# The output projection of a token mixer by seven half products in place of eight

## The chip, the cores and the metric

The kernel runs on one core of one Trainium2 chip. The metric is device time in microseconds (us) of one execution; the median of three runs before the change is 2330.8 us (2329.96 to 2331.77). Everything below counts on one core's engines: TensorE (PE, matmuls), VectorE (DVE), ScalarE (ACT), GpSimd (POOL), SyncE (SP, which issues the DMAs), and the DMA engines.

## The reference

Two layers of a streaming encoder, 512 tokens by 1024 channels in float32. Each layer is a feed-forward net (FFN), a token mixer, and another FFN, each with a norm before and after it. What the change touches is the end of the mixer:

```python
branches = jnp.stack([sb_out, conv_out, gla_out], axis=2)
branch_d = jnp.einsum('bsgw,gwd->bsgd', branches, w_branch)
gates = jax.nn.sigmoid(gate_logits.reshape(b, s, N_BRANCHES, D_MODEL))
merged = jnp.sum(gates * branch_d, axis=2)
return merged @ w_out
```

`merged` is 512 x 1024 and `w_out` 1024 x 1024. Then follow `x = x + rms_norm(m, norm_post[l, 1])` and the second FFN, whose last step is a product with `w_down` (2816 x 1024).

## The kernel before, in words

**Precision.** Each float32 operand is split into a high part (a cast to fp32r, on ScalarE) and a low part (the rest, a subtraction on VectorE). A product is three matmuls: high by high, high by low, low by high. In the names, `whi` and `wlo` are the parts of a weight tile that was loaded as `raw`, `dh` and `dl`, or `mh` and `ml`, those of the other operand. `mm_out` (line 296) issues the three matmuls for 128 tokens by 512 output columns.

**The order of the work.** Matmuls stay in the order of the code. On VectorE and ScalarE, instructions marked `pinned` keep their order among themselves; a scheduler places the rest around them. Each engine's queue is fixed when the kernel is built. `whi` and `wlo` have five buffers each; `raw` has three, each of which holds two loads of 512 KB; and a load is issued by SP, in its order, once its buffer's last reader is done.

**The end of the mixer.** `gates(1, cv, merge)` runs over eight tiles of 128 channels. For each one TensorE computes `gate` (24 matmuls, `proj_cols`) and then `pb` (12 matmuls); ScalarE makes `gs`, the sigmoid of `gate`; VectorE multiplies `pb` by `gs` (line 1210), and GpSimd adds the result to `acc`, the merged tile, which is the transposed operand: 128 channels by 512 tokens. `merge` then splits that tile into `mh` and `ml`. `out_proj` (line 301) multiplies by `w_out`: rows 0 to 511 of the weights (four tiles) one tile after the other into eight PSUM banks, 24 matmuls a tile, then the last four tiles token block by token block (`token(i)`). In that way the first token block's sums are complete early, and the norms of the first blocks run on VectorE and ScalarE while TensorE does the next ones (`Hand`, line 244). Behind the third block come the transposes `pt` of the first normed block for the next FFN.

**The down projection of the FFN** (`Down`, line 569) computes 16 of its 22 weight row tiles by a 2 x 2 block product in seven half products instead of eight. The tokens are halved (`R2` is 0 to 255, `R1` 256 to 511), as are the rows and the columns of the weights. Its table has, for each half product, the operand, the blocks of the weights that are loaded, and the PSUM banks:

```python
        ORDER = (("A12", ((1, 0),), "B"), ("A11", ((0, 0),), "A"), ("S3", ((0, 1), (1, 1)), "C"),
                 ("S2", ((0, 0),), "A"), ("A22", ((1, 0),), "C"), ("S1", ((1, 1),), "A"), ("S4", ((1, 1),), "A"))
```

A step is one half product for a pair of row tiles, 12 matmuls; with 16 tiles there are four steps of each kind (`PER`). `sums(p)` loads the weights of step p and forms its sums on VectorE; `parts(p)` splits both operands, on ScalarE (`dh`, `whi`) and VectorE (`dl`, `wlo`); `ahead()` does the sums of one step and the parts of the step before it. `run` keeps four steps ahead: after product p it prepares step p+4 and, when p was the last of its kind, copies the banks' partial results out (`tap`, ScalarE). The sums `kept` and the copies lie in the buffers of `xh` and `xl`, the stage's input, which is no longer needed then. `MIDDLE` are two ordinary tiles between the sixth and the seventh kind; `LAST` are four that are done token block by token block. `sum_tokens` forms sums of token halves as tiles come; `sum` adds the copied results to the banks at the end.

Of the kernel before, what the change touches and what calls it, by code (L numbers as in the profile page):

```python
# [9 lines left out]
F32R = mybir.dt.float32r  # L10
# [31 lines left out]
def kernel(  # L42
# [33 lines left out]
    def bank(n, tag="pb"):  # L76
        return psp.tile([P, 512], F32, tag=tag, name=n, bufs=BANKS[tag])
# [218 lines left out]
    def mm_out(o, t, sh, sl, wh, wl, st=False, en=False):  # L296
        mm(o, sh[:, t], wh, start=st, stop=False, skip_group_check=True)
        mm(o, sh[:, t], wl, start=False, stop=False, skip_group_check=True)
        mm(o, sl[:, t], wh, start=False, stop=en, skip_group_check=True)

    def out_proj(w2d, nk, stat, tail, finish, upcoming, early, head=None):


        ld = lambda k: load_rows(w2d, k)
        fresh = head is None
        if fresh:
            banks = [[bank(f"o{i}{h}", "pb" if i < 3 else "pa") for h in range(2)] for i in range(NT)]
        else:
            banks, rest = head

        def mms(i, h, k, sh, sl, wh, wl):
            mm_out(banks[i][h], slice(i * P, (i + 1) * P), sh, sl, wh[:, HS[h]], wl[:, HS[h]],
                   fresh and k == 0, k == nk - 1)

        for k in range(nk - tail if fresh else 0):
            wh, wl = ld(k)
            sh, sl = stat(k)
            for i in range(NT):
                for h in range(2):
                    mms(i, h, k, sh, sl, wh, wl)  # L320
        if fresh:
            rest = [(k, ld(k), stat(k)) for k in range(nk - tail, nk)]
        def token(i):
            for h in range(2):
                for k, (wh, wl), (sh, sl) in rest:
                    mms(i, h, k, sh, sl, wh, wl)

        if early is None:
            for i in range(NT):
                token(i)  # L330
                finish(i, banks[i])
            return None

        held[0] = True
        a, b, c, d = [finish(i, banks[i]) for i in range(NT)]
        forms = finish(None, None)
        w, steps = early()
        next(steps)
        token(0)
        a.half(0)  # L340
        a.half(1)
        a.mean()
        token(1)
        a.add()
        b.half(0)
        a.mean()
        b.sum(1)
        a.normal()
        b.square(1)
        b.scaled(1)  # L350
        b.mean()
        token(2)
        c.half(0)
        b.add()
        c.half(1)
        b.mean()
        c.mean()
        arrival(0, a.hns, forms)

        for k, (wh, wl), (sh, sl) in rest:  # L360
            for h in range(2):
                mms(NT - 1, h, k, sh, sl, wh, wl)
        next(steps)
        b.normal()
        for _ in steps:
            pass
        c.add()
        d.sum(0)
        d.sum(1)
        held[0] = False  # L370

        def second():
            held[0] = True
            arrival(1, b.hns, forms)
            held[0] = False
            d.square(0)
            d.square(1)
            c.mean()
            d.mean()
            c.normal()  # L380
            d.scaled(0)
            d.scaled(1)
            d.add()
            d.mean()
            d.normal()

        upcoming.extend((None, second, lambda: arrival(2, c.hns, forms), lambda: arrival(3, d.hns, forms)))
        return w
# [178 lines left out]


    class Down:
        F0, NP = 2, 8  # L570
        R1, R2 = slice(256, 512), slice(0, 256)
        PER = NP // 2

        ORDER = (("A12", ((1, 0),), "B"), ("A11", ((0, 0),), "A"), ("S3", ((0, 1), (1, 1)), "C"),
                 ("S2", ((0, 0),), "A"), ("A22", ((1, 0),), "C"), ("S1", ((1, 1),), "A"), ("S4", ((1, 1),), "A"))
        AHEAD = 4
        MIDDLE, LAST = (0, 1), (18, 19, 20, 21)

        def __init__(self, wd, hid):
            self.wd, self.hid = wd, hid  # L580
            self.ready = {}
            self.s1 = None
            self.next = 0
            self.raw = {}
            self.plan()
# [48 lines left out]
        def sums(self, p):  # L634

            self.load(p)
            j, c = self.steps[p]
            if j is None:
                return
            name, raws = self.ORDER[j][0], self.raw[p]  # L640
            tt = lambda o, a, b, op: pinned(nc.vector.tensor_tensor(o, a, b, op=op))
            kept = None if j < 2 else self.kept[:, 2 * c:2 * c + 2, :].rearrange("p k c -> p (k c)")
            src = raws[0]
            if name == "S3":
                tt(kept, raws[0], raws[1], ALU.subtract)
                src = kept
            if name == "S2":
                for q, x in enumerate(self.of(p)):
                    tt(x, self.s1[c][:, q], x, ALU.add)
                tt(kept, kept, raws[0], ALU.subtract)  # L650
                src = kept
            if name == "S4":
                for q, x in enumerate(self.of(p)):
                    tt(x, x, self.hid[self.F0 + 2 * c + q][:, self.R1], ALU.add)
            if name == "S1":
                pinned(nc.vector.scalar_tensor_tensor(src, kept, -1.0, raws[0], op0=ALU.mult, op1=ALU.subtract))
            if name == "A22":
                tt(src, kept, raws[0], ALU.add)
            self.raw[p] = src
# [40 lines left out]
                    t = slice(q * 256 + i * P, q * 256 + (i + 1) * P)  # L700
                    mm_out(b[i], t, sh, sl, hi[:, w], lo[:, w], st=(q == 0 and c == 0 and j < 3))

        def run(self, late):
            c0, d0, c1, d1, b0, b1 = (bank(n) for n in ("oC", "oD", "oC", "oD", "oB", "oB"))
            a0, a1 = (bank("oA", "pa") for i in range(2))
            self.banks = {"A": (a0, a1), "B": (b0, b1), "C": (c0, c1), "D": (d0, d1)}
            self.out = [[c0, d0], [c1, d1], [b0, a0], [b1, a1]]
# [9 lines left out]
            for p in range(self.end):  # L717
# [12 lines left out]
                if j == 5:  # L730
                    tap(self.u4, "A")
                    for i in range(2):
                        pinned(nc.vector.tensor_tensor(self.u4[i], p7[i], self.u4[i], op=ALU.subtract))

                    self.p1 = [slot("p1") for i in range(2)]
                    for i in range(2):
                        pinned(nc.scalar.copy(self.p1[i], p1[i]))
            while self.next < len(self.steps):
                self.ahead()
            rest = []  # L740
            for p in range(self.end, len(self.steps)):
                sh, sl, hi, lo = self.ready[p]
                rest.append((self.steps[p][1], (hi, lo), (sh, sl)))
            return self.out, rest

        def sum(self, i, h, bank_):

# [24 lines left out]
    def ffn(wg, wu, wd, weights, forms, arrive, finish, upcoming, early, late, begin):  # L772
# [72 lines left out]
        spare.clear()  # L845
        fs = list(range(3, NF))
        n = 7 * len(fs)
        down = Down(wd, hid)
        block_tiles(wg, wu, fs, forms, hid, between)
        head = down.run(late)  # L850
        return out_proj(wd, NF, None, TAIL, lambda i, b: finish(i, b, down.sum), upcoming, early, head)
# [2 lines left out]
    def mixer(l, wv, arrive, finish, upcoming, early):  # L854
# [489 lines left out]
                    nc.vector.tensor_tensor(ys[c], ys[c], s_, op=ALU.mult)  # L1344
                cv = branch_split(ys, "s")

        merged = []

        def merge(d):
            tag = "t" if d < 4 else "q"  # L1350
            mh, ml = slot("mh", F32R, tag), slot("ml", F32R, tag)
            split(mh, ml, acc[d])
            merged.append((mh, ml))

        for _ in gates(1, cv, merge):
            pass
        return out_proj(w_out[l], KC, lambda k: merged[k], TAIL, finish, upcoming, early)


    load_x(0)  # L1360
# [84 lines left out]
```

## Time and profile before

| | |
|---|---|
| median of 3 runs | 2330.8 us |
| profiled execution | 2330.92 us, its span 2329.2 us |
| TensorE, VectorE, ScalarE, GpSimd busy | 99%, 79%, 52%, 7% of the span |
| first matmul of the output projection | 781.8 us (layer 1) |
| its first 168 matmuls, as the chain shows them | 38.08 us |

A row of the groups has line, engine, operation, output<-inputs, shapes and count; behind the bar are the busy time, the mean of one in ns, and the idle time ahead of it with what ended it. A row of a time line has start and length in us. A row of waits has who waited for whom, the total, the number and the longest.

### The profile page before, as it was taken

The page shows a single profiled execution, that of the slowest core. Times are in us where ns is not written, and L with a number is a line of the kernel's source. Part 1 is how long each engine was busy: PE and PEld are TensorE (multiplying, and loading weights), DVE is VectorE, ACT ScalarE, POOL GpSimd, SP SyncE. Part 2 cuts the span into 40 slices and gives each one's busy share as a digit, 9 for nine tenths or more (in the row PEclk, how much of TensorE's full clock was granted, in tenths as well). Part 3 has the DMA queues.
Part 4 walks back from the last instruction along what each step waited for, and adds up shares of the span by engine and source line. Part 5 has one row for each costly group of instructions (what it writes and reads, how often), then busy time and mean ns, then how long its engine had stood idle before and what let it go on. Part 6 is the DMA issues. An engine that isn't in the chain of part 4 may idle for free.

```text
span 2329.2 us, 36177 instructions
## 1 busy us (share of the span) xinstructions
PE 2307.6 (99%) x14072; PEld 2057.9 (88%) x14072; DVE 1848.9 (79%) x2755; ACT 1221.7 (52%) x2370; POOL 165.0 (7%) x277
## 2 busy tenths in 40 slices
PE   8999999999999999999999999999999999999998
PEld 7999888887888899998899998888878888999987
DVE  7888987859965388889888889878599644888897
ACT  5555656644323255556555566566433333566664
POOL 0000001201021100000000000012010211000000
PEclk9999999999999999999999999999999999999999
DMA  5333644131333223336423336432313332333363
GB/s 173 91 109 109 218 161 119 55 100 52 109 91 109 82 73 99 101 109 225 155 82 100 109 110 235 149 110 60 95 55 109 91 92 81 89 99 104 114 221 109
DMA packets 332765, 265.33 MB, mean 114 GB/s; under 512 B 12747, under 2 KB 285165, under 8 KB 332593
## 3 DMA queue, kind: packets, MB, share of 16 engines
q1 hardware_dynamic: 332592, 263.02, 37.2%
q8 instruction: 110, 1.80, 0.3%
q14 instruction: 63, 0.51, 0.1%
HBM read 260.88 MB, written 2.10 MB: 113 GB/s over the span
## 4 chain that ended last, share of the span: by engine, by line
PE 97%; DVE 1%; ACT 1%; issue 0%; DMA 0%; SPq 0%; DVEq 0%; POOLq 0%; ACTq 0%
PE A L66 19%; PE gate L66 11%; PE C L66 9%; PE oA L66 9%; PE pb L66 6%; PE oC L66 5%; PE B L66 5%; PE o L66 3%; PE oB L66 3%; PE pf L66 3%; PE gr L66 2%; PE pa L66 2%; PE q L66 2%; PE gv L66 2%; PE pv L66 2%; PE pgl L66 2%
## 5 line engine op out<-in xcount | busy, mean ns | idle before, releaser
L455 DVE TENSOR_TENSOR wlo<-raw,whi 128x1024 fp32r<-128x1024 f32 (+1 forms) x304 | 331.0, 1089 | 108.7 <-ACT whi L453 107.9
L453 ACT CAST whi<-raw 128x512 fp32r<-128x512 f32 x532 | 315.3, 620 | 162.5 <-DVE raw L455 162.5
L115 ACT CAST whi<-raw 128x1024 fp32r<-128x1024 f32 (+2 forms) x178 | 185.0, 1045 | 351.3 <-PE gate L66 130.8
L116 DVE TENSOR_TENSOR wlo<-raw,whi 128x1024 fp32r<-128x1024 f32 (+2 forms) x178 | 223.0, 1261 | 173.2 <-ACT whi L115 168.5
L455 DVE TENSOR_TENSOR raw<-raw 128x512 f32<-128x512 f32 x304 | 209.1, 688 | 5.7
L66 PE MATMUL A<-xh,whi 128*128 128x256 f32 x608 | 172.5, 284 | 0.0
L66 PE MATMUL A<-xl,whi 128*128 128x256 f32 x608 | 172.0, 283 | 0.0
L66 PE MATMUL A<-xh,wlo 128*128 128x256 f32 x608 | 172.0, 283 | 0.0
L1030 DVE SCALAR_TENSOR_TENSOR y<-u,cw,y 128x511 f32<-128x511 f32 (+14 forms) x240 | 166.5, 753 | 0.0
L66 PE MATMUL gate<-xh,whi 128*128 128x512 f32 x384 | 151.3, 394 | 0.0
L66 PE MATMUL gate<-xh,wlo 128*128 128x512 f32 x384 | 149.8, 390 | 1.3 <-DVE wlo L116 1.3
L66 PE MATMUL gate<-xl,whi 128*128 128x512 f32 x384 | 149.6, 390 | 0.0
L671 ACT CAST whi<-raw 128x1024 fp32r<-128x1024 f32 x104 | 109.5, 1053 | 59.4 <-issue 16.9
L674 DVE TENSOR_TENSOR wlo<-raw,whi 128x1024 fp32r<-128x1024 f32 x104 | 126.6, 1217 | 17.3 <-ACT whi L671 17.3
L268 POOL TENSOR_TENSOR rs<-ms,mhalf 128x1 f32<-128x1 f32 x44 | 25.1, 576 | 1440.6 <-DVE ms L266 1440.6
L453 ACT COPY cp<-A 128x256 f32<-128x256 f32 x228 | 84.4, 370 | 68.5 <-PE A L66 67.6
L66 PE MATMUL oA<-wlo,dh 128*128 128x512 f32 x304 | 119.1, 392 | 0.0
L66 PE MATMUL oA<-whi,dh 128*128 128x512 f32 x304 | 118.4, 389 | 0.0
L66 PE MATMUL oA<-whi,dl 128*128 128x512 f32 x304 | 118.3, 389 | 0.0
L66 PEld LDWEIGHTS A<-xl,whi 128*128 128x128 f32 x608 | 116.5, 192 | 0.2
L66 PEld LDWEIGHTS A<-xh,whi 128*128 128x128 f32 x608 | 116.4, 191 | 0.2
L66 PEld LDWEIGHTS A<-xh,wlo 128*128 128x128 f32 x608 | 116.4, 192 | 0.0
(329 smaller groups left out, 7088.2 us busy)
## 6 DMA issues: line engine op xcount, KB each, us to landing
raw<-in_ffn_w_down_dram SPq DMA_DIRECT2D x152, 512.0 KB, 4.6
raw<-in_w_in_dram SPq DMA_DIRECT2D x108, 512.0 KB, 4.7
raw<-in_ffn_w_gate_dram SPq DMA_DIRECT2D x152, 256.0 KB, 3.4
raw<-in_ffn_w_up_dram SPq DMA_DIRECT2D x152, 256.0 KB, 4.6
raw<-in_w_branch_dram SPq DMA_DIRECT2D x24, 512.0 KB, 3.8
raw<-in_w_out_dram SPq DMA_DIRECT2D x16, 512.0 KB, 4.1
raw<-in_ffn_w_gate_dram SPq DMA_DIRECT2D x12, 512.0 KB, 4.9
raw<-in_ffn_w_up_dram SPq DMA_DIRECT2D x12, 512.0 KB, 4.5
```

Of the source, the lines that this page charges most:

```text
L66: tc.keep_in_program_order(nc.tensor.matmul(*a, **k))
L115: pin(nc.scalar.copy(hi, src))
L116: pin(nc.vector.tensor_tensor(lo, src, hi.bitcast(F32), op=ALU.subtract))
L268: nc.gpsimd.tensor_tensor(self.rs, ms, mhalf[:, 0:1], op=ALU.pow)
L453: copy = lambda o, i: pin(nc.scalar.copy(o, i))
L455: tt = lambda o, a, b, op: pin(nc.vector.tensor_tensor(o, a, b, op=op))
L671: pinned(nc.scalar.copy(hi, src))
L674: pinned(nc.vector.tensor_tensor(lo, src, hi.bitcast(F32), op=ALU.subtract))
L1030: nc.vector.scalar_tensor_tensor(y[:, back:], u[:, :S - back], cw[:, c, j:j + 1], y[:, back:], op0=ALU.mult, op1=ALU.add)
```

## The change

The mixer's output projection now uses `Down` for the first four of its eight row tiles of `w_out`: one step of each of the seven kinds (`NP` is 2, `PER` is 1), no `MIDDLE`, and tiles 4 to 7 as `LAST`. The split of each merged tile in `merge` is gone; in its place come sums of token halves at tiles 2 and 3, and one call of `ahead()` at tile 6. The other steps are prepared in `run`, behind the last gate tile. Since there is no middle tile, six matmuls of the first `LAST` tile are done ahead of the seventh product, and left out later. With one step of each kind, a second place in `kept` holds the later sums. Loads of `w_out` go from 8 to 12 a layer, and its matmuls from 192 to 180. The FFN's calls pass the old numbers.

```diff
-            banks, rest = head
+            banks, rest, done = head
 
         def mms(i, h, k, sh, sl, wh, wl):
+            if not fresh and k == done and i < 2 and h == 1:
+                return
...
     class Down:
-        F0, NP = 2, 8
...
-        PER = NP // 2
...
-        MIDDLE, LAST = (0, 1), (18, 19, 20, 21)
-
-        def __init__(self, wd, hid):
+
+        def __init__(self, wd, hid, f0, np, middle, last):
             self.wd, self.hid = wd, hid
+            self.F0, self.NP, self.PER = f0, np, np // 2
+            self.MIDDLE, self.LAST = middle, last
...
-            kept = None if j < 2 else self.kept[:, 2 * c:2 * c + 2, :].rearrange("p k c -> p (k c)")
+            kept = last = None
+            if j >= 2:
+
+                at = lambda n: self.kept[:, n:n + 2, :].rearrange("p k c -> p (k c)")
+                last = at(2 * c)
+                kept = at(2) if self.PER == 1 and j > 2 else last
...
-                tt(kept, kept, raws[0], ALU.subtract)
+                tt(kept, last, raws[0], ALU.subtract)
...
-        def run(self, late):
-            c0, d0, c1, d1, b0, b1 = (bank(n) for n in ("oC", "oD", "oC", "oD", "oB", "oB"))
+        def run(self, late, order=("C0", "D0", "C1", "D1", "B0", "B1")):
+            got = {n: bank("o" + n[0]) for n in order}
+            c0, d0, c1, d1, b0, b1 = (got[n] for n in ("C0", "D0", "C1", "D1", "B0", "B1"))
...
+                    if not self.MIDDLE:
+
+                        sh, sl, hi, lo = self.ready[self.end]
+                        for i in range(2):
+                            mm_out(self.out[i][1], slice(i * P, (i + 1) * P), sh, sl, hi[:, HS[1]], lo[:, HS[1]], st=True)
...
-        merged = []
+
+        down = Down(w_out[l], acc, 0, 2, (), (4, 5, 6, 7))
+        down.pairs()
 
         def merge(d):
-            tag = "t" if d < 4 else "q"
-            mh, ml = slot("mh", F32R, tag), slot("ml", F32R, tag)
-            split(mh, ml, acc[d])
-            merged.append((mh, ml))
+            for n in range(2):
+                down.sum_tokens(d, n)
+            if d == KC - 2:
+                down.ahead()
 
         for _ in gates(1, cv, merge):
             pass
-        return out_proj(w_out[l], KC, lambda k: merged[k], TAIL, finish, upcoming, early)
+        head = down.run(lambda: None, ("B0", "B1", "C0", "C1", "D0", "D1"))
+        return out_proj(w_out[l], KC, None, TAIL, lambda i, b: finish(i, b, down.sum), upcoming, early, head)
```

The order on VectorE around the last gate tile, before. Tile 7's weights are `raw_7606` in `wlo_7609`; `gs_7477` is tile 4's product, `gs_7528` tile 5's, `gs_7585` tile 6's and `gs_7637` tile 7's; the other `wlo` are those of `w_out`:

```order
L116 TENSOR_TENSOR wlo_7609<-raw_7606,whi_7608 128x1024 [waits DMAHW5_49,PE_49,Activation_49]
L1210 TENSOR_TENSOR gs_7477<-pb_7479,gs_7477 128x512 [waits PE_49,Activation_49]
L116 TENSOR_TENSOR ml_7495<-acc_6487,mh_7494 128x512 [waits Activation_49]
L116 TENSOR_TENSOR wlo_7668<-raw_7606,whi_7667 128x1024 [waits DMAHW6_49,PE_49,Activation_49]
L1210 TENSOR_TENSOR gs_7528<-pb_7530,gs_7528 128x512 [waits PE_49,Activation_49]
...
L1210 TENSOR_TENSOR gs_7585<-pb_7587,gs_7585 128x512 [waits PE_49,Activation_49]
L116 TENSOR_TENSOR ml_7603<-acc_6603,mh_7602 128x512 [waits Activation_49]
L116 TENSOR_TENSOR wlo_7757<-raw_7754,whi_7756 128x1024 [waits DMAHW1_49,PE_49,Activation_49]
L1210 TENSOR_TENSOR gs_7637<-pb_7639,gs_7637 128x512 [waits PE_49,Activation_49]
```

The same place now, up to the third product. `gs_7566` is tile 6's product and `gs_7627` tile 7's; `wlo_7599` are tile 7's weights; `dl_7587` and `wlo_7589` belong to the first half product (A12), `dl_7659` and `wlo_7661` to the second (A11); `xh_7652` is `kept`, written by the sums S3 and S2:

```order
L1222 TENSOR_TENSOR gs_7566<-pb_7568,gs_7566 128x512 [waits PE_49,Activation_49]
L679 TENSOR_TENSOR dl_7587<-acc_6334,dh_7586 128x256 [waits Activation_49]
L679 TENSOR_TENSOR dl_7587<-acc_6410,dh_7586 128x256 [waits Activation_49]
L680 TENSOR_TENSOR wlo_7589<-raw_7583,whi_7588 128x1024 [waits DMAHW5_49,Activation_49]
L116 TENSOR_TENSOR wlo_7599<-raw_7596,whi_7598 128x1024 [waits DMAHW7_49,Activation_49]
L1222 TENSOR_TENSOR gs_7627<-pb_7629,gs_7627 128x512 [waits PE_49,Activation_49]
L642 TENSOR_TENSOR xh_7652<-raw_7596,raw_7655 128x1024 [waits DMAHW1_49,DMAHW0_49]
L679 TENSOR_TENSOR dl_7659<-acc_6172,dh_7658 128x256 [waits Activation_49,Pool_49]
L679 TENSOR_TENSOR dl_7659<-acc_6247,dh_7658 128x256 [waits Activation_49]
L680 TENSOR_TENSOR wlo_7661<-raw_7583,whi_7660 128x1024 [waits DMAHW6_49,Activation_49]
```

Tile 7's `wlo` moved from ahead of tile 4's product to behind tile 6's, and the operands of the second half product stand behind tile 7's product.

On ScalarE, behind the last gate tile, casts of weights stood before, each for a tile of `w_out`:

```order
L115 CAST whi_7785<-raw_7754 128x1024 [waits DMAHW2_49,PE_49]
L115 CAST mh_7654<-acc_6658 128x512 [waits Pool_49]
L115 CAST whi_7791<-raw_7789 128x1024 [waits DMAHW3_49,DVE_49,PE_49]
L115 CAST whi_7796<-raw_7789 128x1024 [waits DMAHW4_49,DVE_49,PE_49]
L115 CAST whi_7802<-raw_7800 128x1024 [waits DMAHW5_49,DVE_49,PE_49]
```

Now the products' casts and the copies stand there. `whi_7711` is cast from the sum of A22, `whi_7737` from that of S1; `xl_7653` holds the copies (`tap`), first of the banks `oA` after the second product, then of the banks `oC` after the third:

```order
L676 CAST dh_7709<-acc_6334 128x256 [waits PE_49]
L676 CAST dh_7709<-acc_6410 128x256
L677 CAST whi_7711<-raw_7682 128x1024 [waits DMAHW3_49,DVE_49,PE_49]
L676 CAST dh_7735<-S1_7224 128x512
L677 CAST whi_7737<-raw_7682 128x1024 [waits DMAHW4_49,DVE_49,PE_49]
L720 COPY xl_7653<-oA_7650 128x512 [waits PE_49]
L720 COPY xl_7653<-oA_7651 128x512 [waits PE_49]
L676 CAST dh_7758<-acc_6334 128x256 [waits DVE_49]
L676 CAST dh_7758<-acc_6410 128x256 [waits DVE_49]
L677 CAST whi_7760<-raw_7731 128x1024 [waits DMAHW5_49,Activation_49]
L720 COPY xl_7653<-oC_7646 128x512 [waits PE_49]
L720 COPY xl_7653<-oC_7647 128x512 [waits PE_49]
```

The copy of the second product's result stands behind the cast for the sixth. In the second layer the rows of these places are alike, with other buffer numbers.

More of the change, by code (lines that the diff above doesn't have):

```diff
@@ L743, in run @@
                 rest.append((self.steps[p][1], (hi, lo), (sh, sl)))
-            return self.out, rest
+            return self.out, rest, None if self.MIDDLE else self.LAST[0]
         def sum(self, i, h, bank_):
@@ L847, in ffn @@
         n = 7 * len(fs)
-        down = Down(wd, hid)
+        down = Down(wd, hid, 2, 8, (0, 1), (18, 19, 20, 21))
         block_tiles(wg, wu, fs, forms, hid, between)
```

## The prediction

> **What bounds the kernel now.** I read the page's list of busy time and its chain first, then TensorE's waits, then the time line of the stage that changes.
>
> ```profile
> PE 2307.6 (99%) x14072; PEld 2057.9 (88%) x14072; DVE 1848.9 (79%) x2755; ACT 1221.7 (52%) x2370; POOL 165.0 (7%) x277
> PE 97%; DVE 1%; ACT 1%; issue 0%; DMA 0%; SPq 0%; DVEq 0%; POOLq 0%; ACTq 0%
> ...
> PE pt L71 <- DVE hn L223: 7.7, 1, 7.7
> PE pf L66 <- ACT xh L115: 2.1, 3, 1.7
> ```
>
> TensorE is busy 99% of the span and makes up 97% of the chain that ended last. Its longest wait is the 7.7 us before its first transpose; the next group is 2.1 us in three. So a matmul taken away is worth its spacing, and any new wait of TensorE is added to the time in full: there is no slack to take it up. The stage that changes is this, in the first layer (chain in order of time: start, length, what):
>
> ```profile
> 773.82 5.44 PE gate L66 x24
> 779.26 2.72 PE pb L66 x12
> 781.98 38.08 PE o L66 x168
> ```
>
> The last gate tile takes 24 + 12 matmuls, then `o`, the output projection, runs without a gap. 38.08 / 168 = 0.227 us is the spacing of its 512-column matmuls, and 36 of them give 8.16 us for a gate tile.
>
> **What goes away.** Half products replace 96 matmuls by 84 in each layer: 12 x 0.227 = 2.72 us, in two layers 5.44 us. All of it is on TensorE's path.
>
> **What is added around it.** Before, each tile was prepared by one cast and one subtraction, long before use. Now seven operand pairs are formed by sums and then split. The down projection of the FFN already runs this code, so its rows price each piece:
>
> ```profile
> L674 DVE TENSOR_TENSOR wlo<-raw,whi 128x1024 fp32r<-128x1024 f32 x104 | 126.6, 1217 | 17.3 <-ACT whi L671 17.3
> L673 DVE TENSOR_TENSOR dl<-hid,dh 128x256 fp32r<-128x256 f32 x192 | 72.3, 417 | 0.9 <-ACT dh L670 0.6
> L1210 DVE TENSOR_TENSOR gs<-pb,gs 128x512 f32<-128x512 f32 x32 | 22.0, 689 | 18.4 <-PE pb L66 18.4
> L671 ACT CAST whi<-raw 128x1024 fp32r<-128x1024 f32 x104 | 109.5, 1053 | 59.4 <-issue 16.9
> L670 ACT CAST dh<-hid 128x256 fp32r<-128x256 f32 x192 | 69.1, 406 | 24.4 <-DVE hid L641 24.3
> L713 ACT COPY xl<-oA 128x512 f32<-128x512 f32 x24 | 12.9, 583 | 0.1
> ...
> 1081.91 0.76 DVE L673 TENSOR_TENSOR dl<-hid,dh 128x256 fp32r<-128x256 f32 x2
> 1082.59 1.22 DVE L674 TENSOR_TENSOR wlo<-xh,whi 128x1024 fp32r<-128x1024 f32 x1
> 1083.72 0.76 DVE L641 TENSOR_TENSOR hid<-S,hid 128x256 f32<-128x256 f32 x2
> 1084.40 1.22 DVE L641 TENSOR_TENSOR xh<-xh,raw 128x1024 f32<-128x1024 f32 x1
> ...
> 1113.28 0.68 DVE L673 TENSOR_TENSOR dl<-S,dh 128x512 fp32r<-128x512 f32 x1
> 1113.88 1.21 DVE L674 TENSOR_TENSOR wlo<-raw,whi 128x1024 fp32r<-128x1024 f32 x1
> ...
> 1058.47 1.06 ACT L671 CAST whi<-raw 128x1024 fp32r<-128x1024 f32 x1
> 1059.43 0.71 ACT L670 CAST dh<-hid 128x256 fp32r<-128x256 f32 x2
> 1060.04 1.05 ACT L671 CAST whi<-raw 128x1024 fp32r<-128x1024 f32 x1
> ```
>
> One such instruction is done after its mean (1.22 us on VectorE for 1024 columns), but the next may start a little sooner. Start to start, VectorE takes 1083.72 - 1082.59 = 1.13 us for 1024 columns, 0.67 for a pair of 256, 0.60 for 512; ScalarE 0.96 for a cast of 1024 and 0.61 for a pair of 256. I use these steps inside a queue, the full duration for whoever waits for the result, and 0.06 us for a hand-over (an estimate from the small gaps between these rows).
>
> **Wait 1: the last gate tile's weights.** Before, VectorE's order has the `wlo` of this tile (`wlo_7609`) ahead of the product of tile 4, and the time line shows such a lead: at 773.93 VectorE multiplies tile 6, just as TensorE begins the last tile, and the `wlo` done before it, at 772.00, already belongs to the output projection.
>
> ```profile
> 772.00 1.23 DVE L116 TENSOR_TENSOR wlo<-raw,whi 128x1024 fp32r<-128x1024 f32 x1 [1.69 <-ACT whi L115]
> 773.93 0.69 DVE L1210 TENSOR_TENSOR gs<-pb,gs 128x512 f32<-128x512 f32 x1 [0.70 <-PE pb L66]
> ...
> 773.66 0.39 PE L66 MATMUL gate<-xh,whi 128*128 128x512 f32 x1
> ```
>
> In the changed order, `wlo_7599` of the last tile stands behind `gs_7566`, the product with tile 6's `pb`, and behind the three splits of the first half product. `gs_7566` waits for the last matmul of tile 6 and starts 773.93 - 773.66 = 0.27 us after TensorE could start the last tile. From that moment: 0.27, then 0.60, 0.67 and 1.13 for the rows ahead, then 1.22 until `wlo` is done: 3.89, with the hand-over 3.95. TensorE needs it for the third matmul, due at 2 x 0.227 = 0.45. It waits 3.5 us. ScalarE's `whi_7598` (behind tile 6's sigmoid and the casts of the first half product) comes at about 0.8 and lies within this.
>
> **Waits 2 and 3: the second and third product.** Call T the moment when the last gate tile's matmuls end and the first product (A12) starts. VectorE's row behind `wlo_7599` is `gs_7627`, which waits for T; everything of the later products stands behind it. It starts at T+0.3. The sum S3 starts at 0.9, the two `dl` of A11 at 2.0, its `wlo` at 2.7 and is done at 3.94. The first product ends at 12 x 0.227 = 2.72 and TensorE can issue one matmul of the second: it waits 4.0 - 2.95 = 1.05 us. Then pair sum (3.85), sum S2 (4.5), `dl` (5.65), `wlo` of S3 (6.3, done 7.55): the second product ends at 6.5, one matmul more, a wait of 0.9. The third ends at 10.1.
>
> **Wait 4: the copy of the first partial result.** The sum for A22 needs a buffer that comes free when `wlo` of A11 has read it, at 3.94; only then does SP issue its load.
>
> ```profile
> raw<-in_w_out_dram SPq DMA_DIRECT2D x16, 512.0 KB, 4.1
> raw<-in_ffn_w_gate_dram SPq DMA_DIRECT2D x152, 256.0 KB, 3.4
> ...
> g<-in_norm_post_dram SPq DMA_DIRECT2D x1, 512.0 KB, 7.7
> ```
>
> With the 4.1 us of the same tensor's loads it lands at 8.1 (VectorE was ready at 7.4). A22 8.1, splits of S2 9.2 and 9.9, the sum S1 from 11.0 to 12.26. ScalarE's queue has `whi_7737`, the cast of S1, ahead of the two copies that take the first result out of bank A, so the copies wait for that sum although their data is there since 6.5: cast 12.3 to 13.4, first copy done at 13.85. The fourth product adds into bank A, so TensorE waits from 10.1 to 13.9: 3.8 us. Queued behind it on ScalarE are the casts of S4 and the copies of bank C, done at 16.6, just when the fourth product ends (16.63). From here TensorE is the later one: the second copies of A (19.1, needed 19.4), the last ones (23.0, needed 23.5) and the last `wlo` (27.4, needed 28.2) are in time. Sum of waits in a layer: 3.5 + 1.05 + 0.9 + 3.8 = 9.3 us. Lower bound: a load of 3.4 us, 8.7 (the queue decides); the upper one, 7.7 us as for `g`, gives 12.9 (a rival below). I take 9.3, since the 4.1 row is the same tensor.
>
> The other additions cost nothing while these waits last: the four pair sums at tiles 2 and 3 lie in VectorE's idle time before `gs` (0.70 us in the row above, against 0.67 for a pair), and the four added loads of 512 KB start behind the others on SP and are needed last; without that cover each sum would be 0.42 us of VectorE.
>
> **The hand-over to the FFN.** Its first transposes wait for the normed first token tile. Sums of partial results come ahead of it (one instruction of 0.69 us a half), as at the end of the FFN. TensorE's waits there, FFN to FFN first, then mixer to FFN:
>
> ```profile
> PE pt L71 <- DVE hn L290: 0.7, 1, 0.7
> PE pf L66 <- DVE xl L116: 0.5, 1, 0.5
> ...
> PE pt L71 <- DVE hn L290: 0.6, 1, 0.6
> ```
>
> The mixer's hand-over has two waits of 0.2 more, 1.0 in all, against 1.2. The second token's block also has three matmuls less, since they are done earlier, so the same chain is met 0.68 us sooner. I take +0.9 us a layer, with 0 and 1.9 as bounds (all hidden; twice the transposes' 0.6 and the 0.7 above).
>
> **The sum.** In a layer -2.72 + 9.3 + 0.9 = +7.5 us, in two +15.0. The profiled execution took 2330.92 us (span 2329.2, 1.7 around it), within 0.1 of the median of the runs, 2330.8. Predicted: 2345.8 us. Its own range: 2 x (8.7 - 2.72) = +12 to 2 x (9.3 - 2.72 + 1.9) = +17, widened by 2 us at each end for the rounding of the steps: 2341 to 2350.
>
> **Rivals.** *No new wait (not slower).* The FFN runs the same products without TensorE standing:
>
> ```profile
> 1057.00:1145.00 88.00, 88.00 (x389) 72.03 (x388) 82.85 (x121) 55.87 (x94) 0.00 (x0) 1.00 0.66 225
> ```
>
> TensorE is busy all of these 88 us, VectorE 82.85. If the mixer kept that pace: 2330.8 - 5.4 + 1.8 = 2327.2. Against it: there four steps are prepared while the gate and up tiles still run and each kind has four steps in a row, so a copy has three products' time; here one step is prepared early and each kind comes once. The decisive point is the two rows `gs_7566` and `gs_7627`: only if the work behind them were done before them could this hold. 5%.
>
> *Only one large wait.* If the last gate tile's `wlo` or the copies came in time, one of 3.5 or 3.8 us a layer falls away: 2345.8 - 7.3 = 2338.5. For it: VectorE is only 79% busy. Against: both follow from in-order queues. 12%.
>
> *The matmuls after a wait run slow.* After the 7.7 us at the start, 256-column matmuls stood 0.21 us apart, then 0.12:
>
> ```profile
> 17.16 0.41 PE L66 MATMUL pf<-wlo,xh 128*128 128x256 f32 x1
> 17.37 0.41 PE L66 MATMUL pf<-whi,xl 128*128 128x256 f32 x1
> ...
> 18.74 0.28 PE L66 MATMUL pf<-whi,xl 128*128 128x256 f32 x1
> 18.86 0.28 PE L66 MATMUL pf<-whi,xh 128*128 128x256 f32 x1
> ```
>
> Here it lasted from the first transposes until 17.6, some 6 us of `pf` work at 0.12 / 0.21 of the pace, a loss of 2.7 us. If the 3.8 us wait sets this off in both layers: 2345.8 + 5.4 = 2351.2. No wait between 0.7 and 7.7 us is in the trace, so it can't say. 10%. The Trainium skill (TensorE: Matmul & The Clock Gate, "Part 1: The HAM clock gate") states the mechanism: the array falls back to half its clock after a whole idle window of about 3.4 us, and the windows run freely; the start of this trace agrees (0.21 against 0.12). By that rule the wait of 3.8 us would set it off only if a window happened to lie wholly inside.
>
> *A late load.* With 7.7 us from issue to landing, wait 4 grows by 3.6: 2345.8 + 7.2 = 2353. Four loads are issued together, but the same tensor shows 4.1. 5%.
>
> **How the numbers follow.** My forecast has 68%, the others 5, 12, 10 and 5. 2338 to 2352 takes in my own range, the single large wait and the slow clock, and leaves out some 10%. A change below 0.2% (4.7 us) can't be told from none. Only the first rival lies there or below: slower 0.94, same 0.04, faster 0.02.
>
> **What would show it.** TensorE's waits should name `gate` or the gate line's `wlo` with some 3.5 us twice, `oA` behind a ScalarE copy with 3.8 twice, and two smaller ones behind `wlo`; 24 matmuls fewer in the count. Wrong if the gate's `wlo` ends before tile 6 does, if the copies precede the cast of S1, or if `o*` products after the long wait are spaced above 0.227.

## The result: 25 us slower, 10 us more than forecast

| | before | changed |
|---|---|---|
| median of the runs beside each other, us | 2330.97 | 2356.41 (2354.43 to 2358.0) |
| ratio, 95% interval | | 1.0109 (1.0091 to 1.0126) |
| profiled execution: time and span, us | 2330.92, 2329.2 | 2358.0, 2356.3 |

The forecast was 2345.8 (2338 to 2352). The sign was right, the time lies outside the range. The page of the changed kernel, its list of busy time and the engines of its chain:

```profile
PE 2315.5 (98%) x14048; PEld 2059.4 (87%) x14048; DVE 1887.7 (80%) x2819; ACT 1240.8 (53%) x2414; POOL 162.6 (7%) x277
PE 94%; DVE 3%; ACT 1%; issue 1%; DMA 0%; POOL 0%; SPq 0%; DVEq 0%; POOLq 0%; ACTq 0%
```

There are 24 matmuls fewer (14072 before) and yet TensorE is busy 7.9 us longer (2307.6 before): matmuls themselves became slower. Its share of the chain fell from 97% to 94%. The waits of TensorE (for whom, total us, times, longest) over the whole span:

```profile
PE gate L66 <- DVE wlo L116: 8.5, 4, 3.6
...
PE oA L66 <- ACT xl L720: 5.1, 2, 2.9
PE oA L66 <- DVE wlo L680: 3.9, 2, 1.9
...
PE gate L66 <- ACT whi L115: 1.0, 2, 0.5
PE oC L66 <- DVE wlo L680: 0.6, 1, 0.6
```

All four places of the forecast are there: the last gate tile's `wlo` (3.6 in each layer; the other two of the row's four have 1.3 in all, as before the change), the second product (`oA` behind `wlo`), the third (`oC`, in one layer), and the fourth (`oA` behind the copies `xl`). Now the chain of the first layer, in order of time (start, length, what):

```profile
779.74 8.13 PE gate L66 x22
...
795.47 4.39 PE oA L66 x11
799.85 2.74 PE oC L66 x12
...
803.19 1.04 ACT whi L677
804.23 0.49 ACT xl L720
...
804.77 4.24 PE oA L66 x12
...
812.15 2.72 PE oA L66 x12
```

Twelve matmuls take 12 x 0.227 = 2.72 us, as the last row has it. The 22 of the gate tile should take 4.99 and took 8.13; the `oA` rows took 4.39 (11) and 4.24 (12). In three places the work behind a wait is slow. The table by windows (from:to, length, then busy time and count of PE, PEld (weight loads), DVE, ACT, POOL, then the granted clock, the DMA share and GB/s) shows the clock there; the borders are those at which the clock's own record changes, and steps of the same length between them:

```profile
775.55:778.96 3.41, 0.57 (x2) 0.14 (x2) 3.41 (x5) 0.00 (x0) 1.31 (x1) 1.00 0.00 0
778.96:782.37 3.41, 2.63 (x6) 2.15 (x7) 0.72 (x1) 0.00 (x0) 0.00 (x0) 0.50 0.00 0
782.37:785.79 3.42, 3.42 (x9) 2.63 (x8) 0.00 (x0) 0.00 (x0) 0.00 (x0) 0.50 0.00 0
...
792.62:796.03 3.41, 1.47 (x6) 0.89 (x6) 3.41 (x6) 1.22 (x2) 1.04 (x1) 1.00 0.62 183
796.03:799.44 3.41, 3.41 (x9) 2.65 (x8) 3.41 (x6) 2.18 (x5) 0.00 (x0) 0.50 1.02 351
...
802.86:806.27 3.41, 1.50 (x7) 1.24 (x8) 3.41 (x8) 3.00 (x6) 0.00 (x0) 1.00 0.07 29
806.27:809.68 3.41, 3.41 (x10) 2.63 (x9) 3.41 (x6) 3.41 (x6) 0.00 (x0) 0.50 0.40 100
```

The matmul clock is granted in steps of 3.41 us: the stretches of its record are 3.41, 6.83, 10.24 us long, or more of the same step. In these rows a step at 1.00 in which TensorE worked 1.5 us or less is followed by one at 0.50. Four steps of the first layer are at 0.50 (the second row, in which TensorE still waits, is followed by one more) and three of the second.

**Where the time went.** I added up, for each layer's stretch around the change (740 to 870 and 1900 to 2040 us), how much more than 0.227 us lies from the start of one matmul to the next: apart in the half-rate steps, and everywhere else (the waits; counted so, each is about 0.3 us longer than in the table of waits: with the 1.9 us above the next matmul starts 795.47 - 793.13 - 0.227 = 2.11 late, and the one after it another 0.11).

| us | before | changed | difference |
|---|---|---|---|
| matmuls saved, 24 x 0.227 | | | -5.4 |
| waits, layer 1, hand-over included | 1.5 | 11.2 | +9.8 |
| waits, layer 2, hand-over included | 1.5 | 12.9 | +11.4 |
| matmuls at half rate | 0 | 9.8 | +9.8 |
| the rest (small gaps elsewhere) | | | +1.5 |
| span | 2329.2 | 2356.3 | +27.1 |

The forecast had -5.4 + 20.4 = +15.0, with 18.6 for the waits and 1.8 for the hand-over. The waits came out at 21.2 in all. What it lacked is the 9.8 us at half rate; the 1.5 us of the rest are small gaps that were not followed.

### The profile page after: what moved, and what is told of

Its sections match the earlier page's. It is cut to its first block, busy times and chain, and to the rows that moved or that the text cites. A ratio compares the mean times of both kernels' runs of the same rounds, so it can differ in the third digit from the quotient of the medians.

```text
span 2356.3 us, 36269 instructions
## 1 busy us (share of the span) xinstructions
PE 2315.5 (98%) x14048; PEld 2059.4 (87%) x14048; DVE 1887.7 (80%) x2819; ACT 1240.8 (53%) x2414; POOL 162.6 (7%) x277
## 4 chain that ended last, share of the span: by engine, by line
PE 94%; DVE 3%; ACT 1%; issue 1%; DMA 0%; POOL 0%; SPq 0%; DVEq 0%; POOLq 0%; ACTq 0%
PE A L66 19%; PE gate L66 11%; PE oA L66 10%; PE C L66 9%; PE oC L66 6%; PE pb L66 5%; PE B L66 5%; PE oB L66 3%; PE pf L66 3%; PE gr L66 2%; PE pa L66 2%; PE q L66 2%; PE gv L66 2%; PE pv L66 2%; PE pgl L66 2%; PE k L66 2%
## 5 line engine op out<-in xcount | busy, mean ns | idle before, releaser
L457 DVE TENSOR_TENSOR wlo<-raw,whi 128x1024 fp32r<-128x1024 f32 (+1 forms) x304 | 331.2, 1089 | 108.4 <-ACT whi L455 107.6
L115 ACT CAST whi<-raw 128x1024 fp32r<-128x1024 f32 (+1 forms) x162 | 168.1, 1044 | 323.1 <-PE gate L66 134.6
L116 DVE TENSOR_TENSOR wlo<-raw,whi 128x1024 fp32r<-128x1024 f32 (+1 forms) x162 | 203.6, 1266 | 134.0 <-ACT whi L115 129.8
L680 DVE TENSOR_TENSOR wlo<-raw,whi 128x1024 fp32r<-128x1024 f32 x122 | 149.3, 1223 | 18.4 <-ACT whi L677 18.4
L677 ACT CAST whi<-raw 128x1024 fp32r<-128x1024 f32 x122 | 128.4, 1052 | 64.8 <-issue 19.6
L66 PE MATMUL oA<-whi,dh 128*128 128x512 f32 x352 | 139.2, 395 | 5.1 <-ACT xl L720 5.1
L66 PE MATMUL oA<-wlo,dh 128*128 128x512 f32 x352 | 140.0, 398 | 3.9 <-DVE wlo L680 3.9
L66 PE MATMUL oA<-whi,dl 128*128 128x512 f32 x352 | 138.7, 394 | 0.0
```

The source lines that it names most:

```text
L66: tc.keep_in_program_order(nc.tensor.matmul(*a, **k))
L115: pin(nc.scalar.copy(hi, src))
L116: pin(nc.vector.tensor_tensor(lo, src, hi.bitcast(F32), op=ALU.subtract))
L457: tt = lambda o, a, b, op: pin(nc.vector.tensor_tensor(o, a, b, op=op))
L677: pinned(nc.scalar.copy(hi, src))
L680: pinned(nc.vector.tensor_tensor(lo, src, hi.bitcast(F32), op=ALU.subtract))
```

## The experiments

Theory A after the result: the waits stand where they were forecast and are about as long, and what is missing is that TensorE runs at half rate behind each of them. Theory B: the waits themselves cost more than was worked out, and the clock has no part in it. The kernels undo or make one part each; all were timed beside the kernel before.

### Matmuls put into the waits

```diff
+FILL = (15, 8, 3, 12)
...
+                mm(pg, gh[:, 0, :], cur["xl"][:, 0, :], start=False, stop=False)
+                for n in range(FILL[0]):
+                    mm(dm, wb[0][:, 0, :], src[0][0], start=True, stop=True, skip_group_check=True)
...
+                    if self.PER == 1 and p in (1, 2) and q == 0 and i == 0:
+                        mm(b[i], sh[:, t], hi[:, w], start=True, stop=False, skip_group_check=True)
+                        more(FILL[p])
...
```

In a layer 15 matmuls are added in the last gate tile and 8, 3 and 12 at the second, third and fourth product. These 38 write where nothing is read before it is begun anew.

> The changed kernel with 38 added matmuls a layer (15, 8, 3, 12) that stand exactly where TensorE waits: ahead of the third matmul of the last gate tile, behind the first one of the second and third products, and ahead of the fourth product. They write banks that are cleared later, so they add 38 x 0.227 = 8.6 us of work a layer. Theory A (the 10 us beyond the forecast are matmuls at half rate after the waits): the waits stay, but TensorE is not idle in them, so no stretch at 0.43 us spacing is left, and the time falls by about 10 us to 2346 (2343 to 2349), although work was added. Theory B (the waits themselves are longer than worked out, the clock has no part): nothing is gained, 2356 or up to 4 us more where the added matmuls overrun a wait.

Measured: 2348.68 us (2348.09 to 2350.54), ratio 1.0075 (1.0060 to 1.0091); 7.7 us below the changed kernel by the medians and 10.0 by the spans (2346.3), with 76 matmuls more. TensorE's waits and the window of the last gate tile in the first layer:

```profile
PE gate L67 <- DVE wlo L117: 1.7, 4, 0.6
PE gate L67 <- ACT whi L116: 1.0, 2, 0.5
PE oA L67 <- ACT xl L732: 0.2, 1, 0.2
...
775.00:791.00 16.00, 15.75 (x68) 12.33 (x67) 7.80 (x9) 3.81 (x7) 2.70 (x2) 1.00 0.09 26
```

The clock is 1.00 (it fell to 0.50 here in the changed kernel), no matmul of the two layers runs at half rate, and the kernel is faster although TensorE does more. The operands are made by the same work in the same order. So the half rate follows from TensorE standing idle: A holds, B falls. The time is 2.7 us above A's middle and inside its range.

### The last gate tile's weights first (undoes wait 1)

```diff
+                    if g == 1 and dd == KC - 2:
+                        early_w[g, KC - 1] = load_cols(W, C_GATE + g * D + (KC - 1) * P)
```

This stands ahead of tile 6's product and of A12's splits, and tile 7 takes its weights from `early_w`.

> The changed kernel with the weights of the last gate tile loaded and split ahead of the first half product's split: wait 1 undone alone. My step for it (3.5 us a layer, 3.6 + 0.5 in the trace): under theory A the wait and the slow matmuls behind it go, 2 x (4.4 + 2.7) = 14 us, to 2342 (2339 to 2346). Under theory B the wait alone, 2 x 4.4 = 9 us, to 2347.5.

Measured: 2343.75 (2342.2 to 2344.77), ratio 1.0052 (1.0037 to 1.0067), span 2340.5.

```profile
PE oA L66 <- ACT xl L720: 4.5, 2, 2.3
PE oA L66 <- DVE wlo L680: 3.9, 2, 1.9
...
PE gate L66 <- DVE wlo L116: 1.3, 2, 0.6
```

The gate's row is back at the 1.3 it has without the change. In each of the two layers 3.6 + 0.5 of wait are gone, 8.2 in all; the time fell by 12.7 by the medians and 15.8 by the spans. So these waits cost well over their length. The time is inside A's range and 3.7 us under B's 2347.5.

### The copies ahead of the next casts (undoes wait 4)

```diff
                 self.product(p)
-                self.ahead()
+                if self.PER > 1:
+                    self.ahead()
...
                     tap(self.u2, "A")
                     late()
+                if self.PER == 1 and j < 5:
+                    self.ahead()
```

> The changed kernel with each copy of a partial result ahead of the next casts in ScalarE's queue: wait 4 undone alone. My step says that the fourth product then waits for nothing (its wlo is done at T+11.6, the third product ends at T+12.0). Under theory A the wait (2.2 and 2.9 us) and a slow window (1.5 to 1.9 us) go in each layer: about -9 us, 2347.5 (2345 to 2351). Under theory B -5.5, 2351. If the wait stays, the copy was not its cause.

Measured: 2349.21 (2348.46 to 2350.82), ratio 1.0077 (1.0062 to 1.0092), span 2346.7.

```profile
PE oC L66 <- DVE wlo L680: 1.2, 2, 0.6
...
PE oD L66 <- DVE wlo L680: 0.3, 2, 0.2
```

The row of `xl` is gone. 0.9 us came back at `oC` and `oD` (0.6 before this edit), whose casts now stand behind the copies. So the order of the copies was the cause of wait 4. The time is inside A's range and 1.8 us under B's 2351, but it does not price this wait cleanly. In the account at the end of the experiments 2.4 us less are waits and 6.5 us less are half rate, and not all of the latter belongs to wait 4: wait 1 is as long as it was, yet one slow step follows it in each layer instead of two, and wait 2 of the first layer is followed by none. Where the borders of the steps fall was luck here.

### The kernel before with one late weight (makes wait 1 alone)

```diff
+            if g == 1 and d == KC - 1:
+                held[0] = True
             pg = proj_cols(W, C_GATE + g * D + d * P, "gate")
+            held[0] = False
...
-                        nc.vector.tensor_tensor(sg, pb, sg, op=ALU.mult)
+                        made = nc.vector.tensor_tensor(sg, pb, sg, op=ALU.mult)
+                        if g == 1 and dd == KC - 2:
+                            pinned(made)
```

Nothing of the block product is in it; with `held` the last tile's splits keep their place behind tile 6's product.

> The kernel before, with one thing changed: the last gate tile's weights are split behind the product of tile 6, as in the changed kernel. One wait alone, without half products. VectorE also has the split of tile 6 in front, so the wait should be 3.5 to 5 us a layer. Theory A: plus 2 to 3.5 us of half-rate matmuls a layer, +11 to +17 in all, 2345. Theory B: the wait alone, +7 to +10, 2339.5.

Measured: 2345.55 (2345.05 to 2346.7), ratio 1.0060 (1.0043 to 1.0077), span 2345.0. The wait, and the clock behind it:

```profile
PE gate L66 <- ACT whi L115: 7.7, 2, 3.9
...
776.60:783.50 6.90, 5.03 (x11) 3.54 (x12) 5.32 (x5) 4.41 (x5) 0.18 (x1) 0.51 0.24 61
783.50:790.00 6.50, 6.50 (x30) 5.37 (x30) 1.70 (x2) 2.32 (x3) 0.00 (x0) 1.00 0.72 258
```

The input that comes last is `whi` here, not `wlo`: on ScalarE it stands behind the split of tile 6's sum. 7.7 us of waits made the kernel 14.5 us slower by the medians, as A had it (B: 8.5). This is the price of such a wait by itself, without the block product: it counts about double.

### GpSimd's sums moved to VectorE

One row of the changed kernel was not explained by order: the pair `dl` took 1.82 us instead of the 0.67 to 0.76 of the forecast's rows. VectorE's and GpSimd's time lines of the changed kernel:

```profile
774.98 0.69 DVE L1222 TENSOR_TENSOR gs<-pb,gs 128x512 f32<-128x512 f32 x1 [7.47 <-PE pb L66]
775.59 1.82 DVE L679 TENSOR_TENSOR dl<-acc,dh 128x256 fp32r<-128x256 f32 x2
...
775.81 1.31 POOL L1223 TENSOR_TENSOR acc<-acc,gs 128x512 f32<-128x512 f32 x1 [6.87 <-DVE gs L1222]
791.52 2.14 POOL L1223 TENSOR_TENSOR acc<-acc,gs 128x512 f32<-128x512 f32 x1 [14.40 <-DVE gs L1222]
```

The pair ends at 777.41, 0.3 us behind GpSimd's sum of tile 6 (775.81 + 1.31 = 777.12). Its first instruction took 0.41 us; the second, which began 0.1 us after GpSimd's, took 1.49, as if it had started its work only when GpSimd was done.

```diff
-                        nc.gpsimd.tensor_tensor(acc[dd], acc[dd], sg, op=ALU.add)
+                        if g == 1 and dd >= KC - 2:
+                            nc.vector.tensor_tensor(acc[dd], acc[dd], sg, op=ALU.add)
+                        else:
+                            nc.gpsimd.tensor_tensor(acc[dd], acc[dd], sg, op=ALU.add)
```

> The changed kernel, but the sums of the gated tiles 6 and 7 into acc are made by VectorE instead of GpSimd. Theory G (GpSimd and VectorE hinder each other): the pair dl that took 1.82 us beside GpSimd's add goes back to the 0.75 us it has elsewhere; VectorE has an add of about 0.6 us more in its queue ahead of the last gate tile's low half, so the wait there falls from 3.6 to about 3.1 us and that ahead of the second product from 1.9 to about 1.4 us; with the clock as it was, 2355 us (2352 to 2357), and up to two half-rate windows of 1.7 us less if a wait falls below the 1.9 us at which windows were halved: not under 2348. Rival N (the pair is slow for its own operands): the pair stays at 1.8 us, the waits grow by the 0.6 us of the add, and the time is 2357 us or more.

Measured: 2354.91 (2354.46 to 2355.22), ratio 1.0099 (1.0085 to 1.0113), span 2353.1.

```profile
774.98 0.69 DVE L1224 TENSOR_TENSOR acc<-acc,gs 128x512 f32<-128x512 f32 x1
775.59 0.75 DVE L679 TENSOR_TENSOR dl<-acc,dh 128x256 fp32r<-128x256 f32 x2
...
PE gate L66 <- DVE wlo L116: 7.8, 4, 3.3
PE oA L66 <- ACT xl L720: 5.8, 2, 2.9
PE oA L66 <- DVE wlo L680: 3.2, 2, 1.6
```

The pair is back at 0.75 and the time inside the range of theory G; rival N falls. The waits behind VectorE fall by 0.3 to 0.4 us each. `oA` behind the copies takes 0.7 of it back, since the product ahead of it ends earlier and the copies do not, and `oC` 0.6 more (1.2 in both layers, 0.6 before).

### Both orders undone, then VectorE's queue filled ahead

Four steps, one on the other. First the last tile's weights and the copies together, by the two edits shown above:

> The changed kernel with the last gate tile's weights loaded and split ahead of A12's halves, and with the copies of banks A ahead of the next casts on ScalarE. Theory A (the loss is waits plus half-rate windows that follow them): the weights alone left a span of 2340.5 us with 4.5 us of waits for the copies in it; without these 2336, plus up to 2 us that the later casts give back to the second and third products' waits; 2338 us (2335 to 2341). Rival M (the waits only move: what is taken from the copies' wait comes back in full at the next products): 2342 us or more.

Measured: 2338.01 (2335.84 to 2339.55), ratio 1.0026 (1.0016 to 1.0036), span 2337.8; A's middle, so the waits did not only move (rival M). This run holds an accident that tells more than its time. The same wait ahead of the second product, 1.95 us by the time line in both layers, is followed by half rate in the first layer and not in the second. The steps of the clock's grid around it, first layer (two rows), second layer (two):

```profile
786.13:789.55 3.42, 1.47 (x7) 0.93 (x6) 3.42 (x6) 1.23 (x3) 0.92 (x1) 1.00 0.00 0
789.55:792.96 3.41, 3.41 (x10) 2.66 (x9) 3.41 (x5) 2.05 (x5) 0.00 (x0) 0.50 0.76 256
...
1943.24:1946.65 3.41, 2.58 (x12) 1.80 (x10) 3.41 (x5) 1.05 (x1) 2.14 (x1) 1.00 0.00 1
1946.65:1950.06 3.41, 2.30 (x10) 1.92 (x11) 3.41 (x6) 1.17 (x3) 0.00 (x0) 1.00 0.26 86
```

In the first layer the wait lies within one step (TensorE busy 1.47 of it), in the second it is cut in two (2.58 and 2.30), and the clock stays at 1.00. So not the wait's length decides but how much of it falls into one step.

Then A11's splits as well, at tile 6, behind those of A12:

```diff
...
             if d == KC - 2:
                 down.ahead()
+                down.parts(1)
+                down.split.add(1)
```

> As the run before, and A11's halves are made as soon as its six tiles are there, ahead of the last gate tile's own work on VectorE. Theory A: the wait ahead of the second product (3.9 us in two layers) goes too, no wait reaches 1.9 us, TensorE stays at full clock, and the time comes down to the waits that are left (0.5 to 1 us a layer at the third product, 0.9 us a layer more at the hand-over) less the 2.72 us a layer of saved matmuls: 2329.5 us (2327 to 2333), which is the kernel before or just below it. Rival V (VectorE has no room: work put ahead of the last gate tile delays that tile's weights or its sums by as much): 2336 us or more.

Measured: 2333.57 (2332.51 to 2335.55), ratio 1.0009 (1.0000 to 1.0018), span 2332.8. The wait ahead of the second product is gone, no step runs at half rate, 2.1 us are left at `oC`. The time is 0.6 us above A's range and 2.4 under V's bound, so A's forecast was missed: of the 8.5 us that it had hoped for, 4.4 came.

The same with the sums of tiles 6 and 7 on VectorE:

> As the run before, with the sums of tiles 6 and 7 into acc on VectorE instead of GpSimd. Theory G: the halves that stood beside GpSimd's add take 0.75 us instead of 1.8 us, the add itself costs VectorE about 0.6 us, so what is left of the waits behind VectorE falls by about 0.5 us a layer: 0.5 to 1 us under the run before. Rival N: 1 us or more above it.

Measured: 2333.42 (2331.62 to 2335.09), ratio 1.0006 (0.9997 to 1.0014). By the profiled executions 1.9 us less (span 2330.9; `oC` 1.3 instead of 2.1), by the medians 0.15 where G had 0.5 to 1: whether it gains anything here stays open.

Last, the third product's operands, made while VectorE waits for the last gate tile's `pb` (`run` then uses this `kept`):

```diff
...
+                    if g == 1 and dd == KC - 1:
+                        down.kept = room("xh", F32)
+                        down.ahead()
+                        down.parts(2)
+                        down.split.add(2)
```

> As the run before with the sums on VectorE, and the third product's operands (S3's weights and halves) are made while TensorE still works on the last gate tile, in the 3.1 us in which VectorE waits for its bank pb. Theory A: the waits ahead of the third product and behind it (1.3 and 0.3 us in two layers by the wait table, 0.3 us more each for the start-up of the matmuls behind it) go; some 1.2 us a layer less than that run's 2333.4: 2331 us (2329 to 2333), no more than 0.1% under the kernel before. Rival V (what is put ahead on VectorE comes back at the fourth and fifth products): 2333 us or more.

Measured: 2329.13 (2327.62 to 2331.36) beside 2330.82 of the kernel before; ratio 0.9991 (0.9982 to 1.0000), span 2328.5. All waits of TensorE in it, except the one at the start:

```profile
PE pf L66 <- ACT xh L115: 2.9, 3, 1.6
PE pt L71 <- DVE hn L290: 2.0, 3, 0.7
PE pf L66 <- DVE xl L116: 1.9, 4, 0.6
PE gate L66 <- DVE wlo L116: 1.3, 2, 0.6
PE oA L66 <- DVE wlo L681: 0.6, 1, 0.6
```

The time is at the lower end of A's range. No product waits in the two mixers (the 0.6 at `oA` lies elsewhere). This is the changed kernel with its operands made in time, and it is level with the kernel before or 0.1% below it: the interval ends at 1. Of the 5.4 us saved the longer hand-over keeps 1.5; some 3 us more lie, in this profile, in gaps of about 0.1 us outside the two mixers' ends, most of them in the FFNs' down projections. The sum of these gaps differs by some 3 us among the eleven profiled executions, and what makes it differ was not followed.

All kernels in the account used above (us, both layers; waits less the 3.0 of the kernel before; to about 0.4, since a matmul that crosses a step's border can be counted on either side):

| kernel | waits and hand-over | half rate | span |
|---|---|---|---|
| changed | 21.2 | 9.8 | 2356.3 |
| waits filled with matmuls (8.6 us of them a layer) | 5.8 | 0 | 2346.3 |
| last weights first | 10.7 | 3.2 | 2340.5 |
| copies first | 18.8 | 3.3 | 2346.7 |
| sums on VectorE | 21.7 | 5.9 | 2353.1 |
| weights and copies | 8.3 | 1.5 | 2337.8 |
| and A11 early | 6.1 | 0 | 2332.8 |
| and sums on VectorE | 5.4 | 0 | 2330.9 |
| and S3 early | 1.5 | 0 | 2328.5 |
| before, one late weight | 8.9 | 5.0 | 2345.0 |

## Why the prediction was wrong, by its own steps

**What goes away: right.** 24 matmuls fewer, 0.227 us each.

**The four waits: right in place and in sum, not each by itself.** By the table of waits, in a layer:

| wait | forecast | layer 1 | layer 2 |
|---|---|---|---|
| 1, last gate tile | 3.5 | 3.6 + 0.5 | 3.6 + 0.5 |
| 2, second product | 1.05 | 1.9 | 1.9 |
| 3, third product | 0.9 | 0 | 0.6 |
| 4, copies | 3.8 | 2.2 | 2.9 |
| sum | 9.3 | 8.2 | 9.5 |

Waits 1 and 2 were forecast too short by the `dl` pair: it was priced at the 0.67 of rows in which GpSimd stood still, and here GpSimd's sum ran beside it (1.1 us more each time). In the second layer wait 3 is 0.6 for 0.9. In the first the second product ran at half rate (4.39 us for 11 matmuls, to 799.85), S3's `wlo` was done at 799.03, and nothing was left of the wait. Wait 4 is shorter because the third product ended later than forecast, at 802.6, which is 12.0 after the first product's start instead of 10.1 (that start is 779.74 + 8.13 + 2.72 = 790.6), while the copies came nearly as forecast, at 804.7, 14.1 after it (forecast 13.85). They came on time although `dl` took longer, because VectorE did not wait for A22's load: the forecast has it idle from 7.4 to 8.1, and in the time line it works without a break from 790.68 until the sum S1 ends:

```profile
797.82 1.21 DVE L680 TENSOR_TENSOR wlo<-xh,whi 128x1024 fp32r<-128x1024 f32 x1
...
801.89 1.22 DVE L662 SCALAR_TENSOR_TENSOR raw<-xh,raw 128x1024 f32<-128x1024 f32 x1
```

The sum of the waits held because waits 2 to 4 share one end, the copies: what the earlier ones take, the last one lacks. In the first layer the half rate itself ate part of waits 3 and 4, so there the nearness of the sum is partly luck. The queue order named in the forecast, the copies behind the cast of S1, is the one in the chain's rows (803.19, just behind the end of that sum at 803.11), and taking the copies first removed the wait.

**The hand-over: right.** In the first layer (760 to 870 us):

```profile
PE pt L71 <- DVE hn L290: 0.7, 1, 0.7
PE pf L66 <- ACT xh L115: 0.6, 1, 0.6
...
PE pf L66 <- DVE xl L116: 0.5, 1, 0.5
```

1.8 us against 1.0 before, +0.8 where +0.9 was taken.

**The step that failed: a wait was priced at its length.** The prediction says that any new wait of TensorE "is added to the time in full", and its sum, -2.72 + 9.3 + 0.9 in a layer, has no term for what the matmuls behind a wait cost. That was left to a rival, "The matmuls after a wait run slow", with 10%, tied to one wait, the 3.8 us one, at 2.7 us a layer. Measured: three waits in the first layer and two in the second set it off, of 1.9 us upward by the table, and it cost 6.1 and 3.7 us, 9.8 in all. The prediction's own sign of being wrong, `o*` products spaced above 0.227 us, is in the chain: the 12 matmuls behind the copies took 4.24 us.

The reason for the small chance was that "No wait between 0.7 and 7.7 us is in the trace, so it can't say". That is not quite so: the prediction's own list has one of 1.7 us, `pf` behind `xh`. It lies at 11.4 us, in the first stretch of the kernel, where matmuls stand 0.21 us apart before and behind it, so it could not say either. The other reason was the rule of the Trainium skill put beside it (TensorE: Matmul & The Clock Gate, "Part 1: The HAM clock gate"), which wants a whole idle window. An unknown price for four waits that were forecast to sum to 9.3 us belonged into the range. Half rate for one step of 3.41 us behind each of the two long waits alone is 2 x 1.7 us a layer, 2352.6 in all, and the range ended at 2352 as if that could not be.

The other rivals: that no new wait arises is what the last kernel above shows for other orders, not for this one; both long waits arose, so the rival with only one of them is out; and a late load took no part, since VectorE stood still for none up to S1.

## What to carry to other kernels

A new wait of TensorE in a dense stretch of matmuls costs its own length and what the lowered clock adds; here a wait of 3.9 us a layer cost 7.2. The shortest wait that set off the half rate was 1.9 us, and the two of 1.6 did not (in the run with the sums on VectorE). So price waits of about 1.7 us and more, half a step, at double until a trace of that kernel says otherwise. Matmuls put into such a wait, even useless ones, won 7.7 us here; to break it in two was not tried; once, by chance, it left the clock at 1.00. Where an operation saves work on the bounding engine by forming operands elsewhere, look first at the in-order queue that forms them: here the seven half products came level with the kernel before only when the operands of the first three stood ahead of the last gate tile's product on VectorE.

## What the runs showed of the hardware

**The clock is decided step by step, on about half a step of work.** In the eleven profiled executions I took TensorE's busy time (as the profile shows it, with modelled ends of the matmuls) in each step of 3.41 us between 30 and 2320 us, some 670 steps each. Of the steps at full clock, the 16 with 1.62 us or less were all followed by a step at half clock, and all the others, 1.75 us the least, by one at full clock: the border lies between 47% and 51% of a step. From half clock, four steps with up to 2.79 us of work stayed at half, and the 16 with 2.83 or more returned. The two rows nearest to the first border, both of the changed kernel; behind the first the clock was 0.50, behind the second 1.00:

```profile
1942.90:1946.32 3.42, 1.62 (x6) 0.68 (x5) 2.43 (x4) 1.35 (x2) 1.31 (x1) 1.00 0.00 0
...
1959.96:1963.38 3.42, 1.75 (x8) 1.13 (x6) 3.42 (x4) 1.05 (x1) 1.89 (x1) 1.00 0.38 108
```

The Trainium skill (TensorE: Matmul & The Clock Gate, "Part 1: The HAM clock gate") has the free-running window of 3413 ns and the two rates, and the trace agrees with both (3.41 us, 1.00 and 0.50). It has the fall back to half rate after an idle window; here a half idle one was enough, and the measurement decides. The changed kernel's four runs had mean granted clocks of 0.994 to 0.996 and spread over 3.6 us, the slowest with the lowest clock; that where the steps fall makes this spread is likely, but only one of the four has a profile.

**GpSimd and VectorE take turns.** The pair `dl` of 256 columns, each instruction with two operands, took 1.82 us beside a GpSimd sum instead of 0.75; and a GpSimd sum that began while VectorE added two operands took 2.14 instead of 1.31. The Trainium skill (SBUF — State Buffer, "SBUF: two separate sides") states it: such a VectorE instruction and a GpSimd one share a port pair that one of them holds for its whole instruction. The run with the sums on VectorE agrees.
